# Attention's queries and keys projected ahead of its values, and a planner with other costs for transfers

## The chip, the core and the metric

The kernel runs on one core of a Trainium2 chip. The metric is the device time in microseconds of one execution, as a median over runs. Engines are named as in the profile: PE (TensorE, with PEld for its weight loads), DVE (VectorE), ACT (ScalarE), POOL (GpSimd) and SP (SyncE, which issues most transfers).

## What is computed

One layer of a hybrid backbone over 512 latent tokens with 256 context tokens, width 1024, in float32. Cut to the parts that the change touches:

```python
h_x = modulate(rms_norm(x, mix_pre_norm), shift, scale)      # and the same for ctx
cq, ckv, kr, z, xbc, dt = in_split(h @ w_in)                 # one input projection
q_nope, q_rope = mla_queries(cq_x, q_norm, w_q_up)           # 16 heads, 64 + 32
k_nope_x, v_x = mla_keys_values(ckv_x, kv_norm, w_kv_up)     # 64 + 64 a head
k_nope_c, v_c = mla_keys_values(ckv_c, kv_norm, w_kv_up)
attn_x = softmax([k_c, k_x] . q * scale) @ [v_c, v_x]        # queries of the latents only
ssd_x = bidirectional Mamba-2 scan of conv(xbc), dt          # chunks of 128, gated with z
x = x + gate * rms_norm(concat(attn_x, ssd_x) @ w_out)
x = x + gate * rms_norm(conv_glu(modulate(rms_norm(x)), w_up, w_down))
```

## The kernel before

**Products.** Each float32 product is made of three products of rounded halves: an operand is split into a high part (a copy on ACT, L597) and a low part (a difference on DVE, L598), and `gemm_T` (L862) multiplies high by high, high by low and low by high. A weight is loaded by SP (L589) into a raw tile and split into two more.

**Stages.** The modulation and z come first (L706, L794), then the input projections. `xbc(m)` (L862) makes one of twelve blocks of 128 columns for the state-space part: products into two double banks, a convolution of five taps on DVE (L888, L892), a tanh, and six transposes on PE (L907). `latent` makes the compressed queries and keys, with a norm (L944, L954). From there two lines of work run beside each other. One is `ssd`, the state-space part: chunk states (L1130), decay products (L1145, which DVE reads at L1151 and L1153), outputs of the chunks (L1168, L1176). The other is `projections`: the rest of the input projection (`rest_of_in`), then attention by pairs of heads. A pair is projected by `project(hp)`: the values for four pairs at once where hp is a multiple of four (six products of six matmuls, L1231, each copied out by ACT at L1233), the rotary queries for two pairs at once (L1241 copies them out), then the pair's queries and keys (L862). Transfers on SP put the pieces together (L1270 to L1277). Then come scores (L1296), softmax (L1298, L1300), transposes (L1312) and the weighted sum (L1324). After attention come the output projection (L1426), the up projection (L862) with the gate (L1553 to L1567), and the down projection (L1660), which is done as seven half-size products of sums and differences. Their right sides are differences of quarters of the down weights, made on DVE (L1653) from loads into six half-block buffers, and one kind is added up by a transfer that POOL issues (L1643).

**PSUM.** The eight banks are handed out by kind with `bk.cut`. During the input projections the double banks 0 to 3 are of kind a and banks 4 and 5 of kind b. `projections` cuts them twice: for the first pair all of banks 0 to 6 are of kind p, and then attention has 0 to 2 for scores, 3 for outputs, 4 and 5 for transposes, and bank 6 alone for projections (p). Bank 7 is the state-space part's.

**The order of the work.** The instructions are recorded once, and a planner (`Graph`, `plan`) then sets the order on each engine and the place of every buffer. It knows a price for each instruction and for each wait between engines; it runs a list of ranks forwards and backwards, keeps the best, and then moves ranks at random `TRIES` times (`refined`), keeping what its own clock calls no slower. The last order found is what the engines run. Of a transfer it assumes that it begins `DMA_START` ns after it is issued, 600 ns more on queues other than SP's, and that an engine other than SP is held for 60 ns by an issue.

## Time and profile before

| what | us |
|---|---|
| median of three runs | 959.47 (958.15 to 961.94) |
| the profiled execution | 960.75 |
| its span, first to last instruction | 959.0 |
| mean granted clock of PE | 0.997 |
| transfers, mean over the span | 143 GB/s |

The profile is one execution, the span a little shorter than its time. Busy times are shares of the span; PE counts as busy while its pipeline holds a matmul, so a busy PE can still run below its peak. A wait is put down to the engine whose work ended last before it. Names of lines (L862) are those of the kernel before.

### The profile page before, as it was taken

To read this page: it belongs to the slowest core of one execution; us is meant where nothing else is said; L and a number is where in the kernel's file an instruction comes from. 1 tells how busy PE (TensorE), PEld (TensorE's weight loads), DVE (VectorE), ACT (ScalarE), POOL (GpSimd) and SP (SyncE) were. 2 spreads that over 40 slices of the span, in tenths; PEclk is the share of its full clock that TensorE was granted. 3 is DMA by queue.
4 is the path that set the end of the run, shared out by engine and by line. 5 is a ranking of instruction groups with operands and counts; after the bars stand their busy time and mean duration, and the time that the engine had idled before them with its cause. 6 is when DMAs were issued, how large, how long until landed. Compare 5 with 4: busy or idle time off the path is not lost.

```text
span 959.0 us, 14661 instructions
## 1 busy us (share of the span) xinstructions
PE 938.5 (98%) x5116; PEld 799.8 (83%) x5116; DVE 751.4 (78%) x1378; ACT 526.9 (55%) x1038; POOL 245.0 (26%) x258
## 2 busy tenths in 40 slices
PE   8999999999999999999999999999999999999996
PEld 8888888887787888898898888988888888878785
DVE  6999787898969998987999976845245376589898
ACT  4465235745677778788985335634133042256674
POOL 0001000748467654823001000000001028240021
PEclk9999999999999999999999999999999999999999
DMA  9943003012322341635567965332234333675774
GB/s 348 347 163 119 31 23 104 24 44 63 81 73 63 98 115 42 158 100 127 173 208 243 363 237 176 112 131 91 74 103 151 132 133 102 150 197 164 246 251 175
DMA packets 54586, 137.53 MB, mean 143 GB/s; under 512 B 8032, under 2 KB 11120, under 8 KB 54512
## 3 DMA queue, kind: packets, MB, share of 16 engines
q1 hardware_dynamic: 52128, 132.03, 42.5%
q0 software_dynamic: 1584, 2.88, 1.8%
q10 hardware_dynamic: 800, 1.68, 0.5%
q8 instruction: 40, 0.66, 0.3%
q14 instruction: 34, 0.28, 0.1%
HBM read 114.50 MB, written 6.34 MB: 126 GB/s over the span
## 4 chain that ended last, share of the span: by engine, by line
PE 79%; DVE 11%; DMA 4%; issue 3%; ACT 2%; POOL 1%; SPq 0%; DVEq 0%; POOLq 0%; ACTq 0%
PE banks L862 39%; PE banks L1426 9%; PE banks L1296 6%; PE banks L1660 5%; DVE block L598 4%; PE banks L794 4%; PE banks L1324 4%; PE banks L1312 3%; DMA block<-in_wdn_dram 2%; PE banks L1231 2%; PE banks L1176 1%; PE banks L706 1%; PE banks L1168 1%; PE banks L1130 1%; ACT block L597 1%
## 5 line engine op out<-in xcount | busy, mean ns | idle before, releaser
L862 PE MATMUL banks<-block,block 128*128 128x512 f32 (+1 forms) x2132 | 449.5, 361 | 1.5 <-ACT block L597 0.8
L862 PEld LDWEIGHTS banks<-block,block 128*128 128x128 f32 x2132 | 358.3, 188 | 61.8 <-ACT block L597 1.0
L597 ACT ACTIVATE block<-block 128x512 fp32r<-128x512 f32 (+4 forms) x329 | 208.5, 670 | 164.6 <-DMA block<-in_wup_dram 31.7
L598 DVE TENSOR_TENSOR block<-block,block 128x512 fp32r<-128x512 f32 (+3 forms) x305 | 239.9, 821 | 37.1 <-ACT block L597 27.7
L1660 PE MATMUL banks<-block,block 128*128 128x512 f32 x462 | 108.4, 391 | 3.5 <-DVE block L1669 1.9
L1660 PEld LDWEIGHTS banks<-block,block 128*128 128x128 f32 x462 | 86.1, 188 | 24.5 <-ACT block L597 2.5
L1296 PE MATMUL banks<-block,block 128*128 128x512 f32 (+1 forms) x384 | 100.7, 358 | 0.7 <-ACT block L1300 0.5
L1426 PE MATMUL banks<-block,block 128*128 128x512 f32 x384 | 91.4, 392 | 0.2 <-ACT block L1300 0.2
L598 DVE TENSOR_TENSOR block<-banks,block 128x256 fp32r<-128x256 f32 (+1 forms) x156 | 83.4, 554 | 8.4 <-ACT block L597 6.3
L1426 PEld LDWEIGHTS banks<-block,block 128*128 128x128 f32 x384 | 71.2, 188 | 14.6 <-ACT block L1300 0.4
L597 ACT ACTIVATE block<-banks 128x256 fp32r<-128x256 f32 (+1 forms) x156 | 72.4, 494 | 16.3 <-PE banks L1312 10.4
L1298 DVE TENSOR_REDUCE smalls<-banks 128x1 f32<-128x768 f32 x64 | 60.7, 949 | 12.5 <-PE banks L1296 10.7
L1324 PE MATMUL banks<-block,block 128*128 128x256 f32 x384 | 69.8, 294 | 0.0
L1312 PE MATMUL banks<-cst,block 128*128 128x128 f32 x384 | 68.0, 273 | 0.7 <-DVE block L598 0.6
L1300 ACT ACTIVATE block<-banks,smalls 128x768 f32<-128x768 f32 x64 | 57.7, 901 | 17.8 <-DVE smalls L1298 13.7
L1296 PEld LDWEIGHTS banks<-block,block 128*128 128x128 f32 x384 | 60.7, 190 | 7.2 <-ACT block L1300 1.1
L696 DVE SCALAR_TENSOR_TENSOR block<-block,block 128x1024 f32<-128x1024 f32 x52 | 63.9, 1243 | 0.5 <-ACT block L773 0.4
L892 DVE SCALAR_TENSOR_TENSOR block<-banks,cwh,block 128x510 f32<-128x510 f32 (+3 forms) x88 | 51.9, 620 | 12.8 <-ACT block L888 12.3
L1324 PEld LDWEIGHTS banks<-block,block 128*128 128x128 f32 x384 | 57.3, 189 | 4.7 <-ACT block L597 0.6
L1553 ACT ACTIVATE block<-banks,prm 128x512 f32<-128x512 f32 x22 | 16.8, 775 | 74.8 <-PE banks L862 74.7
L1567 POOL TENSOR_TENSOR block<-block 128x256 f32<-128x256 f32 x11 | 12.1, 1097 | 174.3 <-ACT block L1558 100.5
L1312 PEld LDWEIGHTS banks<-cst,block 128*128 128x128 f32 x384 | 48.0, 141 | 7.5 <-DVE block L598 2.2
(242 smaller groups left out, 1117.4 us busy)
## 6 DMA issues: line engine op xcount, KB each, us to landing
block<-in_wmod_dram SPq DMA_DIRECT2D x48, 512.0 KB
block<-in_wup_dram SPq DMA_DIRECT2D x44, 512.0 KB
block<-in_wdn_dram SPq DMA_DIRECT2D x88, 256.0 KB
block<-block SPq DMA_DIRECT2D x32, 256.0 KB
block<-in_wout_dram SPq DMA_DIRECT2D x16, 512.0 KB
block<-in_wxbc_dram SPq DMA_DIRECT2D x12, 512.0 KB
block<-block SPq DMA_DIRECT2D x40, 128.0 KB
block<-in_wz_dram SPq DMA_DIRECT2D x16, 256.0 KB
```

The source lines that it names most:

```text
L597: act(hi, src, AF.Copy)
L598: (lo_eng or V).tensor_tensor(out=lo, in0=src, in1=hi, op=ALU.subtract)
L696: V.scalar_tensor_tensor(out=junk, in0=wt, scalar=0.5, in1=vec, op0=ALU.mult, op1=ALU.mult, accum_out=acc)
L862: mm(po, lhsT=wf(k, pt[0]), rhs=xf(k, pt[1]), start=(k == 0 and pt == parts[0]), stop=(k == nk - 1 and pt == parts[-1]))
L892: V.scalar_tensor_tensor(out=st[:, lo:hi], in0=pm[:, lo + d : hi + d], scalar=cwh[:, m * 5 + j : m * 5 + j + 1], in1=st[:, lo:hi], op0=ALU ...
L1296: mm(sc[:, o : o + n], lhsT=q_[:, x_, qi * P : (qi + 1) * P], rhs=kk[:, y_, :], start=part == 0, stop=part == 2)
L1298: V.reduce_max(nm, sc[:, :T], axis=AX.X, negate=True)
L1300: act(pe, sc[:, :T], AF.Exp, bias=nm, scale=1.0, accum_out=sum_)
L1312: nc.tensor.transpose((tx if c < NX else tc_)[:, o : o + P], pe[:, s_ : s_ + P], ident)
L1324: mm(po[:, half * 256 : half * 256 + 256], lhsT=vst(c), rhs=rhs, start=(part == 0 and c == 0), stop=(part == 1 and c == NKT - 1))
L1426: mm(po[i][:, nh * 512 : nh * 512 + 512], lhsT=l[lp][:, i * P : (i + 1) * P], rhs=w[wp][:, nh * 512 : nh * 512 + 512], start=(k == 0 and l ...
L1660: mm(po[i], lhsT=l[:, lp, i * P : (i + 1) * P], rhs=w[wp], start=first and q == 0 and n == 0, stop=q == PAIRS[-1] and n == 2, skip_group_c ...
```

## The change

`project` is cut into `values` and `queries_keys`; the second runs first, and hands its tiles over in `keys`. The first pair no longer has seven banks for its projection: attention's own cut of the banks is made ahead of it, so that it uses bank 6, like the other pairs. The branch for m == 99 is never taken. The planner expects 1500 ns in place of 650 to the start of a transfer, for POOL's queue 2500 on top in place of 600, and 1000 ns in place of 60 of POOL's own time for each issue; it makes 1200 tries in place of 1600. No operation is added or left out.

```diff
-TRIES = 1600
+TRIES = 1200
...
-DMA_START, DMA_WAIT, DMA_AHEAD, DMA_ALONE, RUN, FLYING, DMA_FULL, DMA_FILLS = 650, 910, 3000, 0.8, 80, 8, 600, 40000
+DMA_START, DMA_WAIT, DMA_AHEAD, DMA_ALONE, RUN, FLYING, DMA_FULL, DMA_FILLS = 1500, 910, 3000, 0.8, 80, 8, 600, 40000
...
-                began = t + d + DMA_START + (0 if e == SP else 600)
+                began = t + d + DMA_START + (0 if e == SP else 2500 if e == POOL else 600)
...
-                    clock[e] = t + 60
+                    clock[e] = t + (1000 if e == POOL else 60)
...
+            if m == 99:
+                bk.cut(a=[], p=[bank(i) for i in range(4)])
+                yield from queries_keys(0)
+                bk.cut(a=[two(0), two(2)], p=[])
             xbc(m)
-            yield 8 if m < 10 else 5
+            yield 8
...
-    def project(hp):
+    def values(hp):
 
         if hp % 4 == 0:
...
+        vsx, vsc = t4(P, NX, 4, 64, dt=F32R), t2(P, 2, 4, 64, dt=F32R)
...
+        ready[hp] = keys.pop(hp), (vsx, vsc)
+        yield 2.5
+
+    def queries_keys(hp):
+
         if hp % 2 == 0:
             wr_ = weight(a["wqr"][hp // 2], 384, G)
...
-        ready[hp] = list(zip(qt, kx, kcj)), (vsx, vsc)
-        yield 2.5
+        keys[hp] = list(zip(qt, kx, kcj))
+
+    def project(hp):
+
+        if hp not in keys:
+            yield from queries_keys(hp)
+        yield from values(hp)
...
     def projections():
         yield from rest_of_in()
-        bk.cut(a=[], b=[], s=[bank(7)], p=[bank(i) for i in range(7)])
-        yield from project(0)
-        bk.cut(sc=[(0, 768), (768, 768)], o=[bank(3)], t=[bank(4), bank(5)], p=[bank(6)])
+        bk.cut(a=[], b=[], s=[bank(7)], sc=[(0, 768), (768, 768)], o=[bank(3)], t=[bank(4), bank(5)], p=[bank(6)])
```

Since the planner's numbers change, the whole order is found anew. Three places of it follow. In rows of the changed kernel the line numbers are its own: L1235 is L1231 of before (values), L1149 is L1145 (decay products), L1664 is L1653 (differences of down weights), L1292, L1285 and L1290 are transfers that put queries and keys together.

**The first pair.** On PE, where the values of the first four pairs begin. Before, the matmuls of the first two products stand together:

```order
L1231 MATMUL banks<-block_199_1380,block_285_1944 128x512
L862 MATMUL banks<-block_69_470,block_172_1067 128x512
L1231 MATMUL banks<-block_199_1380,block_285_1944 128x512
L1231 MATMUL banks<-block_314_2161,block_285_1944 128x512 x2
L1231 MATMUL banks<-block_199_1380,block_285_1944 128x512 x2
L1231 MATMUL banks<-block_314_2161,block_287_1950 128x512 x2
L1231 MATMUL banks<-block_218_1533,block_287_1950 128x512
L1231 MATMUL banks<-block_314_2161,block_287_1950 128x512
L1231 MATMUL banks<-block_218_1533,block_287_1950 128x512
L1231 MATMUL banks<-block_314_2161,block_287_1950 128x512
```

Now, from the first value product to the beginning of the second:

```order
L1235 MATMUL banks<-block_19_226,block_285_1950 128x512 x3
L1235 MATMUL banks<-block_347_2275,block_273_1822 128x512
L862 MATMUL banks<-block_69_470,block_304_2073 128x512
L1235 MATMUL banks<-block_347_2275,block_273_1822 128x512 x2
L862 MATMUL banks<-block_69_470,block_305_2074 128x512
L862 MATMUL banks<-block_116_693,block_304_2073 128x256
L1149 MATMUL banks<-block_82_520,sel 128x256 x2
L907 MATMUL banks<-cst,block_110_663 128x128
L862 MATMUL banks<-block_116_693,block_304_2073 128x256
L907 MATMUL banks<-cst,block_110_663 128x128
L862 MATMUL banks<-block_116_693,block_305_2074 128x256
L1235 MATMUL banks<-block_19_226,block_285_1950 128x512 x3
```

Before, two products follow each other at once, each in its own bank; now the six matmuls of the first stand among last input projections, and the second begins behind seven rows of other work.

On SP, the loads for the same place (wk, wv, wqr, wqn are the weights of keys, values, rotary queries and queries; gate_rows are z's rows, read back). Before:

```order
L589 DMA block_0_66<-in_wk_dram 128x256
L589 DMA block_184_1201<-in_wxbc_dram 128x1024
L589 DMA block_207_1441<-in_wv_dram 128x512
L589 DMA block_309_2149<-gate_rows 128x512
L589 DMA block_0_66<-in_wv_dram 128x512
L589 DMA block_207_1441<-gate_rows 128x512
L589 DMA block_272_1815<-in_wqr_dram 128x384
L589 DMA block_272_1815<-in_wqn_dram 128x384
L589 DMA block_87_524<-gate_rows 128x512
L589 DMA block_0_66<-in_wk_dram 128x256
```

Now:

```order
L589 DMA block_0_66<-in_wk_dram 128x256
L589 DMA block_106_627<-in_wxbc_dram 128x1024
L589 DMA block_256_1739<-in_wqr_dram 128x384
L589 DMA block_107_643<-gate_rows 128x512
L589 DMA block_80_506<-in_wv_dram 128x512
L589 DMA block_276_1874<-in_wqn_dram 128x384
L589 DMA block_276_1874<-gate_rows 128x512
L1292 DMA block_199_1385<-block_199_1385 64x512
L589 DMA block_276_1874<-in_wv_dram 128x512
L589 DMA block_0_66<-in_wk_dram 128x256
```

The query weights stood behind both loads of value weights, and are now ahead of the first and of the second.

**The down projection's first loads.** On SP, the last loads of up weights (in_wup) and the first quarters of down weights (in_wdn). Before:

```order
L589 DMA block_1016_6435<-in_wup_dram 128x1024
L589 DMA block_1017_6437<-in_wmod_dram 128x1024
L589 DMA block_1114_7175<-in_wup_dram 128x1024
L589 DMA block_1133_7362<-in_wup_dram 128x1024
L589 DMA block_1016_6435<-in_wup_dram 128x1024
L589 DMA block_1016_6435<-in_wdn_dram 128x512 x2
L589 DMA block_1147_7433<-in_wdn_dram 128x512 x2
L589 DMA block_1133_7362<-in_wdn_dram 128x512 x2
```

Now:

```order
L589 DMA block_1091_6999<-in_wup_dram 128x1024
L589 DMA block_1118_7251<-in_wup_dram 128x1024
L589 DMA block_6_84<-in_wup_dram 128x1024
L589 DMA block_1147_7451<-in_wdn_dram 128x512
L589 DMA block_1145_7450<-in_wdn_dram 128x512
L589 DMA block_1147_7451<-in_wdn_dram 128x512
L589 DMA block_1145_7450<-in_wdn_dram 128x512
L589 DMA block_1136_7383<-in_wup_dram 128x1024
L589 DMA block_1118_7251<-in_wdn_dram 128x512 x2
```

All up weights were ahead of the first quarter before; now four quarters are ahead of the last of them.

**The down projection's differences.** On DVE, from the middle of the down projection (L598 are splits of operands, L1653, or L1664 in the changed kernel, the differences that read fresh quarters). Before:

```order
L1653 TENSOR_TENSOR block_1016_6435<-block_1016_6435,block_1147_7433 128x512
L598 TENSOR_TENSOR block_1071_6792<-block_1133_7362,block_1071_6792 128x512
L598 TENSOR_TENSOR block_919_5539<-block_1063_6770,block_919_5539 128x256
L598 TENSOR_TENSOR block_1048_6642<-block_1016_6435,block_1048_6642 128x512
L598 TENSOR_TENSOR block_1120_7234<-block_1080_6910,block_1120_7234 128x256
L598 TENSOR_TENSOR block_1093_6981<-block_1095_7037,block_1093_6981 128x256
L598 TENSOR_TENSOR block_1093_6981<-block_1110_7167,block_1093_6981 128x256
L1653 TENSOR_TENSOR block_1147_7433<-block_1147_7433,block_1133_7362 128x512
L598 TENSOR_TENSOR block_900_5486<-block_1147_7433,block_900_5486 128x512
L1653 TENSOR_TENSOR block_1133_7362<-block_1133_7362,block_1016_6435 128x512
L1653 TENSOR_TENSOR block_1016_6435<-block_1016_6435,block_1147_7433 128x512
```

Now:

```order
L1664 TENSOR_TENSOR block_1147_7451<-block_1147_7451,block_1145_7450 128x512
L598 TENSOR_TENSOR block_901_5509<-block_1145_7450,block_901_5509 128x512
L598 TENSOR_TENSOR block_1122_7257<-block_1147_7451,block_1122_7257 128x512
L598 TENSOR_TENSOR block_1151_7452<-block_1095_7058,block_1151_7452 128x256
L598 TENSOR_TENSOR block_959_5798<-block_1080_6930,block_959_5798 128x256
L598 TENSOR_TENSOR block_959_5798<-block_1063_6785,block_959_5798 128x256
L1664 TENSOR_TENSOR block_1118_7251<-block_1118_7251 128x512
L598 TENSOR_TENSOR block_1011_6393<-block_1025_6516,block_1011_6393 128x256
L598 TENSOR_TENSOR block_1151_7452<-block_1110_7186,block_1151_7452 128x256
L598 TENSOR_TENSOR block_1058_6726<-block_1118_7251,block_1058_6726 128x512
L598 TENSOR_TENSOR block_159_952<-block_1125_7314,block_159_952 128x256
L1664 TENSOR_TENSOR block_1145_7450<-block_1145_7450,block_1147_7451 128x512
```

Between the first and the second difference stood six splits, and now five; between the second and the third stood one, and now four.

## Prediction

> **What bounds the kernel now.** I read the page first, then the busy time of each engine by 24 us stretches, then what TensorE waited for, then the chain of waits at the places where TensorE is idle.

> ```profile
> span 959.0 us, 14661 instructions
> PE 938.5 (98%) x5116; PEld 799.8 (83%) x5116; DVE 751.4 (78%) x1378; ACT 526.9 (55%) x1038; POOL 245.0 (26%) x258
> ```

> TensorE is busy for 938.5 of 959.0 us, so 20.5 us are all that any new order of the same instructions can win. The change adds no instruction and removes none, so I look for where the 20.5 us lie.

> ```profile
> 0.00:24.00 24.00, 21.48 (x144) 20.64 (x145) 16.20 (x46) 11.74 (x21) 0.85 (x8) 1.00 0.94 348
> 216.00:240.00 24.00, 22.50 (x141) 19.25 (x140) 19.60 (x40) 13.87 (x36) 21.13 (x21) 1.00 0.23 67
> 240.00:264.00 24.00, 21.74 (x110) 18.00 (x109) 22.18 (x46) 14.28 (x34) 11.50 (x14) 0.93 0.33 81
> 288.00:312.00 24.00, 22.75 (x144) 18.95 (x142) 22.67 (x39) 18.62 (x40) 18.65 (x20) 1.00 0.25 64
> 840.00:864.00 24.00, 22.13 (x98) 18.02 (x97) 20.76 (x36) 11.89 (x27) 9.93 (x12) 1.00 0.75 186
> 888.00:912.00 24.00, 22.55 (x94) 16.84 (x93) 19.85 (x40) 15.21 (x36) 0.00 (x0) 1.00 0.78 251
> 936.00:960.00 24.00, 15.35 (x68) 12.39 (x66) 19.58 (x50) 10.49 (x25) 3.00 (x2) 0.92 0.46 166
> ```

> Columns are the stretch, then busy time of PE, PEld, DVE, ACT and POOL, the granted clock, the DMA share and GB/s. The first stretch lacks 24.00 - 21.48 = 2.5 us (the first loads), and the last one ends at 959.0 and lacks 23.0 - 15.35 = 7.7 us (the rows behind the last matmul). Both belong to a start and an end that keep the same chain of work. That leaves 20.5 - 2.5 - 7.7 = 10.3 us in the body, and five rows hold 8.3 of it: 1.50 and 2.26 us where the projections go over into attention, 1.25 us just behind, and 1.87 and 1.45 us in the last stage, the down projection. In the third row the clock is 0.93, so another 0.07 x 24 = 1.7 us pass there at half speed; this is time in which PE counts as busy.

> ```profile
> PE banks L1145 <- DVE block L1153: 2.0, 2, 1.8
> PE banks L1660 <- DVE block L1669: 1.9, 1, 1.9
> PE banks L1660 <- ACT block L597: 1.3, 2, 0.7
> PE banks L1231 <- DVE block L892: 0.5, 1, 0.5
> PE banks L862 <- DVE block L954: 0.4, 1, 0.4
> PE banks L862 <- DVE block L892: 0.3, 1, 0.3
> ```

> These are TensorE's own waits (total, times, longest, in us). Three kinds are seen: the state-space part's decay products (L1145) wait for VectorE, the down projection (L1660) waits for operands made from the last weights, and three small waits, 0.5 + 0.4 + 0.3 = 1.2 us, are of the projections (values L1231, others L862) for PSUM banks that the convolution (L892) or the norm (L954) still read.

> **The change part by part.** (1) *Transfers are expected to land later.* What stands behind the two waits of L1660 is shown by the chain and by VectorE's timeline:

> ```profile
> 832.55 4.05 DMA block<-in_wdn_dram
> 837.80 9.30 DMA block<-in_wdn_dram
> ```

> ```profile
> 886.58 0.69 DVE L1653 TENSOR_TENSOR block<-block,block 128x512 f32<-128x512 f32 x1 [0.28 <-DMA block<-in_wdn_dram]
> 892.51 0.69 DVE L1653 TENSOR_TENSOR block<-block,block 128x512 f32<-128x512 f32 x1 [1.14 <-DMA block<-in_wdn_dram]
> 896.31 1.29 DVE L1653 TENSOR_TENSOR block<-block,block 128x512 f32<-128x512 f32 x2 [1.66 <-DMA block<-in_wdn_dram]
> ```

> Quarters of the down weights (256 KB each) took 4.05 and 9.30 us, and VectorE stood still three times for such quarters, 0.28 + 1.14 + 1.66 = 3.1 us, before TensorE ran dry in the 888 row. These are the rows of the quoted order on VectorE (the down projection's differences, L1653, L1664 in the changed file): the waits of 1.14 and 1.66 us are before the second and the third difference in it. Between the first and the second stood six rows of splits, and five in the new order; between the second and the third stood one, and now four. A row of these splits costs

> ```profile
> 897.52 2.29 DVE L598 TENSOR_TENSOR block<-block,block 128x256 fp32r<-128x256 f32 x5
> ```

> 2.29 / 5 = 0.46 us, so the wait of 1.66 us gets 3 x 0.46 = 1.4 us of cover and that of 1.14 us loses 0.46: 0.9 us less lateness, which I pass on to TensorE's 1.45 us of idle time in the 888 row. For the 840 row the order on SP shows four quarters issued ahead of the last up weights, behind which all of them stood before. I count half of its idle time, 0.9 of 1.87 us, since a second reading limits it:

> ```profile
> 836.00:855.00 19.00, 17.03 (x74) 13.43 (x72) 14.10 (x21) 7.21 (x15) 11.65 (x14) 1.00 0.95 243
> ```

> From 836 to 855 us the DMA engines are busy at 0.95. A transfer that waits for other transfers does not land earlier because the plan expects it later; it only does so if it is issued ahead of this stretch, as four of them now are. For the whole of part 1 the bounds are 0 and 1.87 + 1.45 = 3.3 us, and I take 0.9 + 0.9 = 1.8 us won, the middle.

> [...]

> (2) *POOL's transfers are expected to cost its queue more.* Only the eleven accumulating loads of the down projection (L1643) are issued there.

> ```profile
> block<-in_wdn_dram POOLq DMA_DIRECT2D x11, 256.0 KB, 5.6
> ```

> They land 5.6 us after their issue (median). TensorE's waits do not name POOL, and POOL has 14 of 24 us free in the 840 row, so an earlier issue delays no sum of POOL's that is waited for. The term is 0; if the eleven loads crowd SP's in the stretch at 0.95, or land late themselves, that is within the bounds of part 1.

> (3) *Queries and keys of pair 0 first, and on attention's one bank.* Before, the ten products of the first pair (four for queries and keys, six for values) went round seven banks, six of which the convolution and the norm had used just before. The three bank waits of 1.2 us fall away, since bank 6 belongs to neither. Bounds are 0 (another wait ends at the same time) and 1.2, and I take 1.2, as nothing else is named in those rows. SP's queue follows the change: the query weights now stand ahead of or between the value weights, as the order shows, with no load more and none fewer.

> What is added is a wait for the one bank between products. The trace of before shows this price, since the second set of values already runs on it:

> ```profile
> 367.06 1.40 PE banks L1231 x6
> 369.49 1.39 PE banks L1231 x6
> 371.93 1.39 PE banks L1231 x6
> 374.66 1.42 PE banks L1231 x6
> 377.10 1.40 PE banks L1231 x6
> 360.00:384.00 24.00, 24.00 (x152) 20.96 (x152) 21.18 (x66) 21.07 (x51) 10.74 (x14) 1.00 0.13 40
> L1241 ACT ACTIVATE block<-banks x4: 578/594/601, 238.6 to 428.4; 128x512 f32<-128x512 f32 x4
> ```

> Five products of 1.4 us begin 2.44 to 2.73 us apart, (377.10 - 367.06) / 4 = 2.5 us, so about 1.1 us pass between two; 0.59 us of it is the copy out of the bank (the L1241 row has the same shape as the values' copy). TensorE is busy for all 24.00 us meanwhile: scores, transposes and decay products fill the pauses. With cover the price is 0, and without it ten products cost 10 x 1.1 = 11 us. In the new order the first value product (L1235 there) is cut by L862, seven rows of L862, L907 and the decay products (L1149 there) stand between it and the second, so I take 0 and keep 11 as the end of the range. Queued behind a waiting product on TensorE are the first scores, and behind those softmax on ScalarE and VectorE.

> (4) *Fewer tries, the new yield, the branch for m == 99.* They leave no instruction of their own; what they do is in the new order.

> (5) *All else that the new order moves.* The long wait of the decay products, 1.8 us, is not touched by any of these parts. It has a price beyond itself:

> ```profile
> 257.40:260.80 3.40, 1.80 (x6) 1.39 (x7) 3.33 (x10) 2.31 (x7) 2.17 (x3) 0.88 0.79 195
> 260.80:264.20 3.40, 3.40 (x13) 2.69 (x13) 1.77 (x3) 0.97 (x3) 1.27 (x2) 0.62 0.27 91
> ```

> After a stretch with 1.80 of 3.40 us busy, the granted clock falls to 0.62: this is the 1.7 us above. So one such wait costs 1.8 + 1.7 = 3.5 us, and the new order may lose it (down to -3.5) or make another where VectorE is nearly full, as in the 288 row with 22.67 of 24 (up to +3.5). I take 0, the middle, as both orders feed the same work through the same VectorE.

> [...]

> **Sum.** The profiled execution took 960.75 us (a span of 959.0 and 1.75 around it). 960.75 - 1.8 - 1.2 = 957.75. The three timed runs have their median at 959.47, 1.3 below the profiled one; 3.0 us off this gives 956.5, which I predict for the median of the changed kernel.

> **Rivals.** *A: the stall of the decay products goes too.* The rows around that wait stand in another order now, and VectorE has idle time ahead of it (19.60 of 24 in the 216 row). Then 3.5 us more are won, and with the rest of the two rows of the last stage, 3.3 - 1.8 = 1.5, this is 956.5 - 5.0 = 951.5. Against it: VectorE is at 22.18 in the 240 row itself. *B: the change does not do what it says.* The transfers are late because the DMA engines are full (0.95), not because they start late, and a bank wait that goes is replaced by a wait for VectorE, which is as late. Then it gives 959.5. For it speaks that TensorE is at 98%; against it that VectorE waited for transfers by name. *C: slower.* At the first pair, between the projections and the first softmax, nothing covers the pauses of the one bank: the fill of 360 us came from scores and transposes of a pair before, and pair 0 has none. From the point at which more than 3.0 / 1.1 = 2.7 of the ten products stand uncovered it is slower than before. With eight uncovered, and the clock halved once, it is 956.5 + 8.8 + 1.7 = 967.0. Against it: L862 of the last convolution inputs stands between the products in the order.

> **How the numbers follow.** Forecast 0.42, A 0.22, B 0.22, C 0.14. By 0.5%, about 4.8 us and what a measurement can tell from no change, faster means below 954.7 and slower above 964.3. A is faster (0.22), and of the forecast's 0.42 I put 0.11 there, since its upper bounds in parts 1 and 3 reach 956.5 - 1.5 = 955.0 and part 5 may add to it: 0.33. C is slower: 0.14, and 0.02 of B for a further stall: 0.16. The rest is 0.51. The range reaches from a little beyond A, 950.5, to B with one new stall of 3.5 us, 963.0; it leaves out C and the far tail of A, about 0.2.

> **What would show it.** Right: TensorE's idle time in the last 120 us (without the end) falls from 3.3 to about 1.5 us, VectorE's waits for the down weights shrink, and no PE row of values or L862 waits for L892 or L954 near 240 us. Wrong: waits of PE for the copies of bank 6, a second stretch with a clock below 1.00, or the DMA share at 0.95 with the same idle time. If the new order lost time at places that none of the parts names, the working would be wrong even if the total fits.

## The result, and the profile after

The changed kernel takes 954.61 us (median of five runs, 953.1 to 957.41) where the kernel before took 961.26 beside it (958.15 to 963.88). The ratio is 0.9934 with a 95% interval of 0.9906 to 0.9961: 0.4 to 0.9% faster. The profiled execution took 954.86 us with a span of 953.1, 5.9 less than before. These are the page's span and busy times of the changed kernel:

```profile
span 953.1 us, 14651 instructions
PE 938.1 (98%) x5116; PEld 802.4 (84%) x5116; DVE 749.7 (79%) x1378; ACT 526.1 (55%) x1038; POOL 246.2 (26%) x258
```

TensorE's work is the same (938.5 before), so 5.5 of the 5.9 us are idle time that went: 20.5 before, 15.0 now. The busy times by stretch, in the columns of the prediction, show where:

```profile
192.00:312.00 120.00, 118.88 (x711) 102.05 (x710) 107.97 (x200) 79.57 (x177) 82.95 (x75) 0.99 0.27 71
216.00:240.00 24.00, 22.90 (x134) 19.78 (x133) 19.20 (x37) 11.12 (x23) 13.60 (x11) 0.93 0.34 93
240.00:264.00 24.00, 24.00 (x138) 20.83 (x138) 22.98 (x49) 18.97 (x47) 15.58 (x16) 1.00 0.33 87
288.00:312.00 24.00, 23.98 (x142) 19.84 (x141) 22.72 (x36) 17.83 (x38) 22.81 (x21) 1.00 0.20 55
840.00:864.00 24.00, 21.86 (x90) 17.53 (x89) 21.28 (x34) 14.15 (x30) 7.25 (x10) 0.93 0.43 102
888.00:912.00 24.00, 23.36 (x99) 18.00 (x98) 22.87 (x47) 16.59 (x36) 0.00 (x0) 1.00 0.76 246
836.00:855.00 19.00, 16.86 (x68) 13.39 (x67) 17.16 (x23) 8.97 (x19) 8.93 (x11) 0.91 0.55 114
```

From 192 to 312 us TensorE now lacks 120 - 118.88 = 1.1 us, and lacked 5.5 before (its row: 114.49 of 120): 4.4 of the 5.5 us. The 888 row won 0.8. The 840 row, from which the prediction took 0.9, lost: 2.14 us idle in place of 1.87, and a clock of 0.93, although the DMA engines are busy at 0.55 from 836 to 855 us where they were at 0.95. TensorE's two longest waits in these stretches are the old one of the down projection and a new one, of the norm's sum on POOL:

```profile
PE banks L1671 <- DVE block L1680: 2.1, 1, 2.1
PE banks L944 <- POOL block L941: 1.0, 1, 1.0
```

Of the three bank waits on L892 and L954 and of the 2.0 us wait of the decay products none is left.

### The profile page after: what moved, and what is told of

It is laid out like the page before. It is cut to its first block, busy times and chain, and to the rows that moved or that the text cites. A ratio compares the mean times of both kernels' runs of the same rounds, so it can differ in the third digit from the quotient of the medians.

```text
span 953.1 us, 14651 instructions
## 1 busy us (share of the span) xinstructions
PE 938.1 (98%) x5116; PEld 802.4 (84%) x5116; DVE 749.7 (79%) x1378; ACT 526.1 (55%) x1038; POOL 246.2 (26%) x258
## 4 chain that ended last, share of the span: by engine, by line
PE 88%; DVE 7%; ACT 2%; issue 1%; DMA 1%; POOL 0%; SPq 0%; DVEq 0%; ACTq 0%
PE banks L862 43%; PE banks L1437 9%; PE banks L1309 6%; PE banks L1671 6%; PE banks L794 5%; PE banks L1337 4%; PE banks L1325 4%; DVE block L598 3%; PE banks L1235 2%; PE banks L1134 2%; DVE block L1664 1%; PE banks L706 1%; PE banks L1180 1%; PE banks L1172 1%; ACT block L597 1%
## 5 line engine op out<-in xcount | busy, mean ns | idle before, releaser
L862 PE MATMUL banks<-block,block 128*128 128x512 f32 (+1 forms) x2132 | 450.8, 362 | 0.4 <-DVE block L1258 0.3
L862 PEld LDWEIGHTS banks<-block,block 128*128 128x128 f32 x2132 | 359.4, 189 | 61.9 <-issue 1.6
L597 ACT ACTIVATE block<-block 128x512 fp32r<-128x512 f32 (+4 forms) x329 | 208.5, 670 | 150.7 <-DVE block L696 30.3
L598 DVE TENSOR_TENSOR block<-block,block 128x512 fp32r<-128x512 f32 (+3 forms) x305 | 236.3, 809 | 63.4 <-ACT block L597 34.4
L1671 PE MATMUL banks<-block,block 128*128 128x512 f32 x462 | 111.4, 396 | 2.8 <-DVE block L1680 2.1
L1309 PE MATMUL banks<-block,block 128*128 128x512 f32 (+1 forms) x384 | 94.9, 352 | 0.2 <-ACT block L1313 0.2
L1437 PE MATMUL banks<-block,block 128*128 128x512 f32 x384 | 90.5, 391 | 0.0
L598 DVE TENSOR_TENSOR block<-banks,block 128x512 fp32r<-128x512 f32 (+1 forms) x156 | 83.2, 554 | 8.9 <-ACT block L597 8.5
L597 ACT ACTIVATE block<-banks 128x256 fp32r<-128x256 f32 (+1 forms) x156 | 72.1, 496 | 20.1 <-PE banks L1325 13.6
L1309 PEld LDWEIGHTS banks<-block,block 128*128 128x128 f32 x384 | 60.0, 189 | 7.2 <-ACT block L1313 1.9
L1325 PE MATMUL banks<-cst,block 128*128 128x128 f32 x384 | 63.7, 273 | 0.4 <-DVE block L598 0.4
L892 DVE SCALAR_TENSOR_TENSOR block<-banks,cwh,block 128x510 f32<-128x510 f32 (+3 forms) x88 | 53.0, 621 | 9.7 <-ACT block L888 8.9
## 6 DMA issues: line engine op xcount, KB each, us to landing
block<-in_wdn_dram SPq DMA_DIRECT2D x88, 256.0 KB
block<-block SPq DMA_DIRECT2D x32, 256.0 KB
block<-in_wz_dram SPq DMA_DIRECT2D x16, 256.0 KB
```

What stands on the lines that cost most here:

```text
L597: act(hi, src, AF.Copy)
L598: (lo_eng or V).tensor_tensor(out=lo, in0=src, in1=hi, op=ALU.subtract)
L862: mm(po, lhsT=wf(k, pt[0]), rhs=xf(k, pt[1]), start=(k == 0 and pt == parts[0]), stop=(k == nk - 1 and pt == parts[-1]))
L892: V.scalar_tensor_tensor(out=st[:, lo:hi], in0=pm[:, lo + d : hi + d], scalar=cwh[:, m * 5 + j : m * 5 + j + 1], in1=st[:, lo:hi], op0=ALU ...
L1309: mm(sc[:, o : o + n], lhsT=q_[:, x_, qi * P : (qi + 1) * P], rhs=kk[:, y_, :], start=part == 0, stop=part == 2)
L1325: nc.tensor.transpose((tx if c < NX else tc_)[:, o : o + P], pe[:, s_ : s_ + P], ident)
```

## Experiments: one part at a time, and other draws

The planner tries changes at random and keeps those that its model calls no worse, so any edit draws another order for the whole program (one order found in this way is called a draw below). The first eight kernels separate the parts from the draw. **attn_only** is the changed kernel with the old numbers:

```diff
-DMA_START, DMA_WAIT, DMA_AHEAD, DMA_ALONE, RUN, FLYING, DMA_FULL, DMA_FILLS = 1500, 910, 3000, 0.8, 80, 8, 600, 40000
+DMA_START, DMA_WAIT, DMA_AHEAD, DMA_ALONE, RUN, FLYING, DMA_FULL, DMA_FILLS = 650, 910, 3000, 0.8, 80, 8, 600, 40000
...
-                began = t + d + DMA_START + (0 if e == SP else 2500 if e == POOL else 600)
+                began = t + d + DMA_START + (0 if e == SP else 600)
...
-                    clock[e] = t + (1000 if e == POOL else 60)
+                    clock[e] = t + 60
```

**numbers_only** is the kernel before with the same three lines the other way round. Both make 1200 tries.

The names with _s4 or _s5 have another seed and nothing else:

```diff
-        chance = random.Random(3)
+        chance = random.Random(4)
```

What was expected of the four that ran first:

> The changed file with the planner's numbers of before (650; 600 and 60 for POOL), so the attention edit and the fewer tries alone. Edit theory (the gain of 0.66% comes from the queries and keys first and their own bank): 954 to 956, the three bank waits on L892 and L954 gone, idle time of PE between 192 and 312 us near 1 us in place of 5.5. Numbers theory (later transfers win it): 959 to 961, like before. Re-draw theory (any new order wins or loses a few us by which stalls happen to arise): anywhere from 953 to 962; the bank waits gone all the same.

> The kernel before with the planner's new numbers (1500; 2500 and 1000 for POOL) and 1200 tries, without the attention edit. Numbers theory: 955 to 957, less idle time of PE in the rows 840 and 888. Edit theory: 959 to 961, with bank waits on L892 or L954 near 240 us. Re-draw theory: anywhere from 953 to 962.

> The kernel before with another seed of the planner's random tries (4 for 3) and nothing else: the same instructions, another order. Edit and numbers theories: within 1 us of before (960 to 962), since neither edit is in it. Re-draw theory: off by 2 to 5 us to either side, by stalls at other places and halved clocks that come or go (1.7 us each).

> The changed kernel with another seed (4 for 3) and nothing else. Edit and numbers theories: within 1 us of the changed kernel (954 to 956). Re-draw theory: off by 2 to 5 us to either side; if it is as slow as before (960), most of the 0.66% is the draw.

Neither part alone gave anything in its first draw: attn_only took 962.5 us and numbers_only 963.7, where before took 963.1 beside them, and both theories had expected 954 to 957 of their part. The whole change did win twice. That left an interaction or the draw, and four more kernels ran:

> The attention edit with the planner's numbers of before, seed 4 for 3. With seed 3 this was 1.000 of before, while the whole change was 0.993 and with seed 4 0.992. Interaction theory (the edit wins at 192 to 312 us, but a load expected too early makes a new stall elsewhere, 3.3 us at 493 us in the run with seed 3): about 1.000 again (0.997 to 1.003), PE's idle time between 192 and 312 us at 2 to 3 us and at least one stall behind a load. Re-draw theory: 0.993 to 1.003, either.

> The kernel before with the planner's new numbers and 1200 tries, seed 4 for 3. With seed 3 this was 1.000 of before. Interaction theory: about 1.000 again (0.997 to 1.003), VectorE's waits for the down weights near 0, a bank wait of L1231 on L892 of about 1 us still there, 4 us or more of PE's idle time between 192 and 312 us. Re-draw theory: 0.993 to 1.003.

> The changed kernel, seed 5 for 3. Interaction theory: 0.991 to 0.995 of before, as with seeds 3 and 4; no bank waits on L892 or L954, VectorE's waits for down weights below 0.5 us. Re-draw theory: 0.993 to 1.003, and a third draw as fast as two others would have a chance below one half.

> The kernel before, seed 5 for 3. Interaction theory: 0.998 to 1.004 of before, as with seed 4 (1.0019), with VectorE's waits for down weights of 3 us or more and the bank wait of L1231 on L892. Re-draw theory: 0.993 to 1.003.

The table has the ratio to the kernel before, run on the same chip, with its interval, and from the profile of each, in us: TensorE's idle time from 192 to 312 us (120 less its busy time in that row), its bank waits on L892 and L954, the start of the first score product (L1296, L1309 with the edit), VectorE's waits for down weights by name, TensorE's idle time from 816 to 936, and from 312 to 816.

| kernel | ratio (95%) | 192:312 | bank waits | first scores | waits for down weights | 816:936 | 312:816 |
|---|---|---|---|---|---|---|---|
| before | 1 | 5.5 | 1.2 | 262.6 | 6.9 | 3.5 | 0.5 |
| before_s4 | 1.0019 (1.0003 to 1.0035) | 4.2 | 1.5 | 261.2 | 10.1 | 4.2 | 4.7 |
| before_s5 | 0.9966 (0.9951 to 0.998) | 4.7 | 0.9 | 259.7 | 7.9 | 3.6 | 1.7 |
| numbers_only | 1.0 (0.9986 to 1.0014) | 4.6 | 1.1 | 259.8 | 0 | 3.5 | 4.6 |
| numbers_only_s4 | 0.9991 (0.9979 to 1.0003) | 4.4 | 1.4 | 260.0 | 1.7 | 4.0 | 2.7 |
| attn_only | 1.0 (0.9981 to 1.002) | 3.1 | 0.2 | 254.0 | 6.1 | 2.7 | 7.5 |
| attn_only_s4 | 0.9953 (0.9934 to 0.9972) | 2.3 | 0 | 250.8 | 4.5 | 3.7 | 2.7 |
| after | 0.9934 (0.9906 to 0.9961) | 1.1 | 0 | 252.8 | 0 | 2.8 | 1.0 |
| after_s4 | 0.9917 (0.9896 to 0.9938) | 2.0 | 0 | 250.2 | 0.2 | 3.2 | 3.1 |
| after_s5 | 0.9971 (0.9957 to 0.9984) | 2.2 | 0.4 | 251.8 | 0 | 1.1 | 4.8 |

Four things are read from it.

*The draw is as large as the change.* Three seeds of the kernel before lie from 0.9966 to 1.0019, three of the changed one from 0.9917 to 0.9971: 0.5% each, with nothing but the seed between them, and the two ranges overlap. A part of it stands in the last column, stretches that no part of the change speaks of: 0.5 us in before, 4.7 in before_s4. It is not all: before_s5 is faster than before with more idle time in whole (21.7 against 20.5 us), as its matmuls are busy for 933.8 us in place of 938.5. Of these 4.7 us the halved clock of before is 1.7 (0.07 x 24 in its 240 row, an estimate); the rest is not broken down here. The largest idle time of the last column is in attn_only: its row at 494 us, and from ScalarE's timeline the row with which the pause ends:

```profile
494.00:500.00 6.00, 3.26 (x17) 2.90 (x18) 3.00 (x6) 4.89 (x9) 0.00 (x0) 0.81 1.01 368
```

```profile
494.81 1.06 ACT L597 ACTIVATE block<-block 128x1024 fp32r<-128x1024 f32 x1 [3.79 <-issue]
```

TensorE runs for 3.26 of 6 us, ScalarE's split of a 128x1024 operand started after 3.79 us of idle time in which the profile names no engine, and the DMA engines are full (1.01). VectorE's splits behind it, and behind those TensorE, started as late. A load that the order expects too early would look like this; which load it was is not shown.

*The attention edit wins where it was made, in every draw.* From 192 to 312 us the five kernels with it lack 1.1 to 3.1 us, the five without 4.2 to 5.5; the means are 2.15 and 4.66, so 2.5 us. The bank waits are 0.9 to 1.5 us without it and 0 to 0.4 with it, on the mean 1.2 and 0.1, so 1.1 of these 2.5 us. The rest goes with the start of attention. The first score product of before, and of after:

```profile
262.65 1.19 PE L1296 MATMUL banks<-block,block 128*128 128x512 f32 x3
```

```profile
252.83 0.86 PE L1309 MATMUL banks<-block,block 128*128 128x512 f32 x3
```

With the edit scores begin at 250.2 to 254.0 us, without at 259.7 to 262.6, while the decay products still run: TensorE has other work while one of them waits. In the profiles with the edit the waits of the state-space lines in this stretch come to 0, 0, 0, 0.5 and 2.0 us, without it to 0.9 and four times 2.0 to 2.7; the means are 0.5 and 2.1. That the earlier scores are what covers these waits agrees in nine draws of ten, but was not tested by itself.

*The numbers do what they say, and TensorE has little of it.* VectorE waits 4.5 to 10.1 us for down weights with the old numbers and 0 to 1.7 with the new. TensorE's idle time from 816 to 936 falls only from a mean of 3.53 to 2.91 us. One wait that no step of the prediction spoke of goes as well: TensorE's 0.8 us for ScalarE's L749 near 48 us is in all five profiles with the old numbers and in none with the new.

*Interaction.* The means of the ratios are 0.9995 (before, three draws), 0.9996 (numbers, two), 0.9977 (attention, two) and 0.9941 (both, three). With 0.5% between draws of one kernel, only the step from before to both, 0.5%, stands out, and weakly, since the ranges overlap. Of the interaction theory's four ranges for the second four kernels three were missed (attn_only_s4 with 0.9953, after_s5 with 0.9971, before_s5 with 0.9966), while the re-draw theory's range held all four. That both parts are needed is therefore not shown. Taken by the attention edit alone, the five draws with it have a mean of 0.9955 and the five without 0.9995.

## Experiments: the 840 row, in one fixed order

Here the plan of the kernel is taken as it is and a few rows of it are moved by hand, so nothing else is drawn anew. First, what the 840 row of the changed kernel consists of. Of VectorE's groups by form from 846.4 to 849 us (busy time, mean ns):

```profile
L598 DVE TENSOR_TENSOR block<-block,block 128x256 fp32r<-128x256 f32 x1 | 2.8, 2751 | 0.0
```

And from the timelines of VectorE, POOL and TensorE (start, duration, what ended the idle time before):

```profile
849.09 0.41 DVE L1680 SCALAR_TENSOR_TENSOR block<-block,block 128x256 fp32r<-128x256 f32 x1
846.50 1.02 POOL L1577 TENSOR_TENSOR block<-block,block 128x256 f32<-128x256 f32 x1
847.21 1.00 POOL L1578 TENSOR_TENSOR block<-block 128x256 f32<-128x256 f32 x1
847.89 0.99 POOL L1579 TENSOR_TENSOR block<-block,block 128x256 f32<-128x256 f32 x1
849.56 6.61 PE L1671 MATMUL banks<-block,block 128*128 128x512 f32 x21 [2.14 <-DVE block L1680]
```

A split on VectorE took 2.75 us, from 846.4 to 849.2, while POOL worked through three differences of the last pair of up projections (L1577 to L1579); the split behind it (L1680) is what TensorE waited for. So two edits. In **after_sums** and **before_sums** these three rows are issued on VectorE and stand right behind that split in its order:

```diff
+    for i in SITES["sums"]:
+        pool.remove(i)
+    at = dve.index(SITES["behind"][0]) + 1
+    dve[at:at] = SITES["sums"]
```

In **after_quarters** the last up weight goes back ahead of the four quarters on SP's queue:

```diff
+    last = max(sp.index(i) for i in SITES["behind"])
+    early = [i for i in sp[:last] if i in SITES["sums"]]
+    sp[:] = [i for i in sp[: last + 1] if i not in early] + early + sp[last + 1 :]
```

(`SITES["sums"]` holds the loads of quarters here.) And **after_both** is after_sums with the norm's sum (L941) moved to VectorE too:

```diff
+    for i in SITES["norm"]:
+        pool.remove(i)
+        ready = max(end[j] for j in order["Activation"] if j < i and j >= i - 3)
+        dve.insert(next(k for k, j in enumerate(dve) if end[j] > ready), i)
```

> The changed kernel in its own order, without a new draw, but the last pair's three differences for the Strassen-like sums (POOL, lines 1577 to 1579) stand on VectorE, behind the split that TensorE waits for at 849 us. In the profile of the changed kernel VectorE's 128x256 split took 2.75 us in place of 0.41 while POOL ran these three. Contention theory (in the 840 row TensorE waits because VectorE's rows are stretched by POOL's, not because of loads): the split takes 0.4 us, TensorE's idle time in the 840 row falls from 2.14 to below 0.5 us, the halved clock there goes, and the time falls by 2 to 4 us to 0.989 to 0.992 of before. Load theory (late down weights): idle time stays near 2 us, time 0.993 to 0.995.

> The same edit in the kernel before, in its own order: VectorE's splits at 850 to 854 us took 1.2, 1.7 and 1.7 us in place of 0.68 beside POOL's rows. Contention theory: TensorE's idle time of 1.87 us in the 840 row falls below 0.6 us, 0.997 to 0.999 of before. Load theory (as predicted, a quarter of 9.30 us stands behind it): idle time stays near 1.9 us, 0.999 to 1.002.

> The changed kernel in its own order, but on SP's queue the last up weight stands ahead of the four quarters of the down weights, as before the change. Predicted step (these four quarters ahead win 0.9 us in the 840 row): VectorE waits for quarters again by name and TensorE's idle time in the 840 row grows by about 0.9 us, 0.994 to 0.996 of before. Contention theory: the row's idle time stays at 1.9 to 2.4 us, and the time at 0.992 to 0.995.

> As after_sums, and the norm's one sum of squares on POOL (line 941, 2.80 us, for which TensorE waited 1.0 us at 222 us) stands on VectorE. Contention theory: both stalls and the halved clocks behind them go (2.1 + 1.0 us idle, 1.7 us for each clock), 0.986 to 0.990 of before. If a halved clock does not hang on these stalls: 0.990 to 0.992. If VectorE's added row of about 1 us delays another product: no better than after_sums.

The 840 rows of after_sums, before_sums and after_quarters, in this order, with the last one TensorE's row behind its wait, and the split of 2.75 us as it is in after_sums:

```profile
840.00:864.00 24.00, 24.00 (x107) 19.63 (x106) 23.75 (x43) 15.66 (x34) 6.39 (x8) 1.00 0.51 127
```

```profile
840.00:864.00 24.00, 23.85 (x105) 19.41 (x104) 21.86 (x41) 13.31 (x29) 7.38 (x9) 1.00 0.75 193
```

```profile
840.00:864.00 24.00, 21.86 (x97) 17.71 (x96) 23.00 (x39) 14.17 (x31) 5.77 (x8) 1.00 0.44 112
```

```profile
848.08 8.21 PE L1678 MATMUL banks<-block,block 128*128 128x512 f32 x35 [2.14 <-DVE block L1687]
```

```profile
L598 DVE TENSOR_TENSOR block<-block,block 128x256 fp32r<-128x256 f32 x1 | 0.4, 412 | 0.0
```

With POOL's three rows away the split takes 0.41 us in place of 2.75, and TensorE's idle time falls from 2.14 to 0.00 us in the changed kernel, and from 1.87 to 0.15 in the kernel before. With the four quarters put back it is 2.14, to the hundredth what it was. So VectorE's rows, stretched beside POOL's, make this stall in the changed kernel, and the place of the four quarters does not touch it. Nor did VectorE wait for quarters by name in after_quarters, as the predicted step had it: the place of these four is not what took VectorE's waits away. In the kernel before, taking away the stretch was enough to end the stall. A wait of 1.51 us for a quarter, up to 847.20, stands ahead of it on the same path; whether ending that wait would have done as well was not tried. In before_sums VectorE's four splits at 850 us (one of 128x256 and three of 128x512, merged in the row) show the stretch too; they took 4.75 us before:

```profile
849.91 2.75 DVE L598 TENSOR_TENSOR block<-block,block 128x256 fp32r<-128x256 f32 x4
852.59 0.41 DVE L1673 SCALAR_TENSOR_TENSOR block<-block,block 128x256 fp32r<-128x256 f32 x1
```

The times: before_sums 0.9975 of before (0.9963 to 0.9988), 2.3 us between the medians, as the contention theory expected. In the two profiles it is less, 959.0 and 958.1 us, for the 888 row lacks 1.97 us in place of 1.45. after_sums is at 0.9893 (0.9876 to 0.991), but after_quarters, which kept its stall, is at 0.9898 (0.9885 to 0.991), lower than either theory had it. The gain of after_sums is therefore seen in its profile and not in its time. In the profiles the clock differs. The changed kernel (mean clock 0.992) has a clock of 0.93 in the first 24 us, in the 216 row and in the 840 row; after_sums (0.992) has 0.86 in the first 24 us and 0.93 in the 216 row; after_quarters (0.996) has 0.93 in the 216 row alone. A clock of 0.93 over 24 us costs 1.7 us (0.07 x 24, an estimate). So, as far as the profiles show, after_quarters is short by where the clock was halved, and not by its edit. The changed kernel was not run beside these, so for the timed runs this stays open.

In after_both the new wait of the norm goes as well. Its page and its 216 row:

```profile
span 948.2 us, 14648 instructions
```

```profile
216.00:240.00 24.00, 23.66 (x144) 20.54 (x143) 21.86 (x44) 13.44 (x27) 11.75 (x11) 1.00 0.40 111
```

The idle time there falls from 1.10 to 0.34 us and the clock is whole. It takes 950.56 us, 0.9861 of before (0.9845 to 0.9878), against 953.41 for after_quarters on the same chip, and is the fastest of all kernels here.

## Why the prediction was right, point by point

The time, 954.6, lies in the range of 950.5 to 963.0 and 1.9 below the 956.5 that was forecast. The gain was forecast as 3.0 us; it is 6.65 us between the medians and 5.9 in the profile. "Faster by over 0.5%" came true with 0.66%, and had 0.33 against 0.51 for no change.

That the time lies in the range is in part luck. Of the 5.5 us of idle time that went, the stretch from 816 to 936 us gave 0.7 where the sum had 1.8, and the one from 192 to 312 gave 4.4 where it had 1.2; two seeds of one kernel differ by more than the 3.0 us that were forecast. Of the signs that the prediction named, VectorE's waits and the bank waits went as it said. The idle time of the 840 and 888 rows fell from 3.3 to 2.8 us only, not to about 1.5. And a sign of being wrong came: the clock is below 1.00 in two stretches, the 216 and the 840 row, and a wait of 1.0 us, at the norm, stands where no part named one.

**Part 1, transfers.** Half held. The quarters come in time: VectorE's waits for them went from 6.9 us (the table) to none, and the 888 row won 0.8 of 0.9 us. That the one made the other is not shown: numbers_only, with no such wait, lacks 1.46 us in the 888 row, and attn_only, with 6.1 us of them, 0.70. The step that failed is "I count half of its idle time" for the 840 row: nothing was won there. The chain had shown a transfer of 9.30 us that ended at 847.1, and I took it for the cause; it was followed by 7.5 us of VectorE's rows to 854.7, of which about 2 us were stretch beside POOL (four splits took 4.75 us, and 2.75 in before_sums). In the changed kernel no such transfer is waited for, and the stretch alone makes 2.14 us. What counted was the last link ahead of TensorE's wait. The row that gave 0.46 us for a split holds both 128x256 (0.41 us) and 128x512 (0.68).

**Part 2, POOL's queue.** Taken as 0. The two numbers were not tried apart, so this stays open. That TensorE's waits do not name POOL was not so: L787 waits 1.3 us for POOL's L755 in the first 24 us of both kernels, and in the changed kernel the norm waits for POOL too.

**Part 3, queries and keys on one bank.** Right in kind: the bank waits go in three draws of five and shrink to 0.2 and 0.4 us in the others, and the pauses of the one bank cost nothing, since in all five draws TensorE is busy for the whole of the 240 and the 264 row, where the first values stand. It was too small: 1.2 us, where the stretch from 192 to 312 us gives 2.5 on the mean of ten draws and 4.4 in this one. The bank waits themselves were sized well (1.1 us on the mean). What the term left out is that attention begins 9.8 us earlier in this draw.

**Part 4, tries.** Not tried alone.

**Part 5, the rest of the order.** 0 with 3.5 us to either side was about right: three draws of one kernel lie 0.5%, or 5 us, apart. In this draw the wait of the decay products went, as rival A had it, and a new one came at the norm (1.0 us). The 1.7 us, which the prediction calls time at half speed, are what the half speed costs; the spell lasts twice as long: the trace of before has a clock of 0.50 from 259.95 to 263.37 us. Nor are 20.5 us of idle time all that an order can win: the busy time differs by 4.7 us between two draws of the kernel before.

**Rivals.** A's stall went, but the halved clock that was to go with it came at other places (the 216 and the 840 row). B (nothing) holds for either part alone in its first draw. C (slower, no cover) did not come: TensorE is busy for 24.00 of 24 us in the 240 and the 264 row, with last input projections ahead of the first scores and with scores behind them.

## What to carry to other kernels

Where a planner with random tries lays out the program, run an edit with several seeds before believing 0.5% (three were too few to tell 0.5% from the draw here), and look for what every draw shares. Follow a stall to the row that ended last ahead of it and compare that row's length with its usual one: here a row of 2.75 us in place of 0.41 named another cause than the chain's longest link. Edits made by hand in one fixed order tell causes apart that a new draw hides.

## What was not expected of the hardware

VectorE's rows with both inputs in SBUF (`block`) were held up while POOL computed, by up to 3.3 us for a single row: 2.75 us in place of 0.41 for 128x256 above, and in numbers_only 3.75 for the same shape:

```profile
L598 DVE TENSOR_TENSOR block<-block,block 128x256 fp32r<-128x256 f32 x1 | 3.8, 3751 | 0.0
```

In the traces this goes with where the inputs lie. In the trace of the changed kernel 111 splits of 128x512 with both inputs in SBUF run while POOL computes nothing, and none takes over 0.69 us; of the 46 that overlap a computing row of POOL 26 take longer, up to 1.48. The 38 splits of this shape that overlap such a row with one input in PSUM (`banks`) all stay at 0.69 or less.

A halved clock does not follow from a stall's length alone. The wait of 2.14 us in the 840 row was followed by it in the changed kernel and not in after_quarters, whose row above has 1.00. The first row is of the changed kernel, the second of before_sums, whose decay stall is 1.77 us where that of before, 1.78 us, was followed by 0.62:

```profile
849.40:852.80 3.40, 3.24 (x8) 2.56 (x9) 3.00 (x7) 1.26 (x3) 0.00 (x0) 0.50 0.16 30
```

```profile
260.00:263.40 3.40, 2.59 (x11) 2.08 (x12) 3.03 (x7) 2.44 (x6) 1.83 (x3) 1.00 0.55 145
```

```profile
846.02:849.43 3.41, 1.40 (x7) 0.72 (x5) 3.41 (x3) 2.15 (x5) 2.86 (x4) 1.00 0.88 127
```

```profile
844.26:847.67 3.41, 1.68 (x8) 0.96 (x6) 3.41 (x3) 2.07 (x5) 3.13 (x5) 1.00 0.93 151
847.67:851.08 3.41, 3.00 (x13) 2.52 (x14) 3.41 (x9) 2.01 (x5) 0.00 (x0) 1.00 0.04 8
```

The columns are those of the prediction, the third number from the end the clock. In the changed kernel 2.01 us of the stall fall into one stretch (3.41 less 1.40), and the clock is halved in the next, the first of the two rows above; in after_quarters the end of a stretch cuts the stall into 1.73 and 0.41 us, and the clock stays whole. Likewise one stretch of before, from 256.54 to 259.95 us, has TensorE idle for 2.26 us, with a clock of 0.50 in the next, and the two of before_sums that share its stall 0.70 and 1.55, with the clock whole behind them. The norm's wait does not fit: its stretch in the changed kernel, from 221.38 to 224.79 us, has 0.96 us of idle time, and the clock is 0.50 in the next, where before has one with 1.27 us (853.82 to 857.23) and a whole clock behind it. The stretch at the norm holds twelve matmuls of a single column (L944) as well.

By rows of 24 us from 24 to 936 us, the fourteen profiles have 30 rows with over 1.5 us of idle time, and nine of them have a clock below 1.00. Of the other 502 rows three have: the 216 row, with the norm's wait and 1.00 to 1.10 us idle, in three kernels of one order (the changed kernel, after_sums and after_quarters).

So "one such wait costs 1.8 + 1.7 = 3.5 us" was an upper end, not a price. A whole stretch of idle time was not needed: 2.26 and 2.01 us of 3.41 were each followed by a halved clock, 1.73 and 1.55 were not, and at the norm 0.96 were.

The five runs of the changed kernel order by the mean granted clock in the same way: 953.1 us at 0.996, 954.5 and 954.61 at 0.994, 954.86 at 0.992, 957.41 at 0.990.
